# The gate columns of an input projection as Strassen block products: two of seven inside the attention, five behind it

## The chip, the cores and the metric

One core of a Trainium2 chip runs the whole program. The metric is the device time of one execution in microseconds (us). TensorE is called PE below, VectorE DVE, ScalarE ACT, GpSimd POOL and the queue of SyncE SP; every engine works through its own list of instructions in order.

## What is computed

A decoder block over 16 meta tokens and 1024 tokens of width 1024, in float32. The normalized rows h go through one projection `w_in`, whose columns feed a pooling mixer (u, z_pool), an attention of 8 heads (q, k, v, z_attn, forget gates) and two gates of 1024 columns each:

```python
h = rmsnorm(x, norm_g)
proj = einsum('bld,dn->bln', h, w_in)
u_pool, z_pool, q, k, v, z_attn, f_logit, g_pool, g_attn = split(proj)
y_pool = causal_multiscale_pool(u_pool) * silu(z_pool)
y_attn = forgetting_attention(q, k, v, log_f) * silu(z_attn)
merged = sigmoid(g_pool) * (y_pool @ w_up_pool) + sigmoid(g_attn) * (y_attn @ w_up_attn)
out = rmsnorm(x + merged @ w_out, final_norm_g)
```

## The kernel before

**Numbers in two parts.** Every product is taken on float32 operands that are split in a high part (ACT copies it to a shorter format) and a low part (the rest, a subtraction). A product is high·high + high·low + low·high, so a 512-column result over 1024 rows costs 3 × 8 = 24 matmuls of 128x512, and a chunk of 128 output columns for all 1024 tokens costs 48. `split_w` loads such a chunk of the weights (`raw`, two buffers), lets ACT make `whi` and POOL make `wlo` in four pieces of 128x256 (L128). h itself stands transposed and split in `hh` and `hl`.

**Stages.** (1) Norm, transposes and q, k, v of the first pair of heads, 0 to about 67 us. (2) The forget gates and the attention: 16 units (pair p, head e, half of the queries), up to 503.8 us. A unit with the first half of the queries has 5 key blocks, one with the second half 9. Each block has a pair of matmuls for the logits (`ps`, L549, L550), work on DVE, ACT and POOL for the maximum, the exponential, the split (`ph`, `pl`) and the row sums (`acc`), and a pair of matmuls on the values (`po`, L610). (3) Behind the attention: the rest of the projection, the pooling mixer and the two up projections, to 660.8 us. (4) The output projection and the last norm, to 756.4 us.

**What sets the order.** PE's list is written out by hand; the other lists are ordered by the compiler. In the attention PE's list is filled up with work that nothing there needs: `Fill.pull(ns)` inserts matmuls of the q, k, v chunks of the later pairs and of "free" chunks until they are worth `ns` by a small formula. Free are 4 chunks for u and 20 of the 24 chunks of za, zp, gp and ga (`f_raw`, 48 matmuls each; za, zp have 4 chunks each, gp and ga, the gates, 8 each). `f_raw` evacuates each 512 columns with ACT into `st` and stores them to a DRAM tile `sp_...`. The last 4 chunks (`left`) come behind the attention. The gates are needed late: `up_weights` reloads a gate chunk and `up` multiplies the up projection with its sigmoid.

**Names.** `acc` is the row sum of a unit on POOL, `m` the running maximum on DVE, `u` and `s` the tiles of the pooling chain, `y` the attention's result that is reloaded and gated by POOL in `attn_gate`, `rc` the reciprocal row sums, loaded in `attn_out`.

Of the kernel before, what the change touches and what calls it, by code (L numbers as in the profile page):

```python
# [14 lines left out]
D = 1024  # L15
NM = 16
# [14 lines left out]
RESERVE = 4  # L31
PJ, PT = 3, 2
PACE = 2.05
LATENCY = 1800.0
# [7 lines left out]
WARM = (4, 1)  # L42

# [10 lines left out]
def tile_hybrid_block(ctx, tc, x, meta, norm_g, w_in, b_forget, pool_w, pool_scale,  # L54
# [4 lines left out]
    w_in2 = w_in[0].rearrange("(k p) n -> p k n", p=128)  # L59
    wup_p = w_up_pool[0].rearrange("(k p) n -> p k n", p=128)  # L60
# [8 lines left out]
    gp = ctx.enter_context(tc.tile_pool(name="gp", bufs=13))  # L69
# [4 lines left out]
    psT = ctx.enter_context(tc.tile_pool(name="psT", bufs=PT, space=PS))  # L74
    G_, P_ = ExitStack(), ExitStack()
# [41 lines left out]

    def split_w(srcs, pool=None, tags=("wh", "wl")):
# [7 lines left out]
        nc.scalar.activation(hi, raw, AF.Copy)  # L126
        for k in range(0, KO, 2):
            nc.gpsimd.tensor_tensor(lo[:, k:k + 2], raw[:, k:k + 2], r32(hi[:, k:k + 2]), op=ALU.subtract)  # L128
        return hi, lo
# [176 lines left out]

    class Fill:
# [195 lines left out]
    pw = ap_.tile([128, 4, 128], F32, name="pw", tag="ls")  # L503
# [135 lines left out]
    raws = [(n, j) for n, c in (("za", 4), ("zp", 4), ("gp", 8), ("ga", 8)) for j in range(c)]  # L639

    for g in (3, 2, 1, 0):
        F.add_free(f_u(g))
# [37 lines left out]
    A.close()  # L680
    P_.close()

    bp = ctx.enter_context(tc.tile_pool(name="bp", bufs=1, reuse_waits="tile"))
    p8 = ctx.enter_context(tc.tile_pool(name="p8", bufs=3, space=PS, reuse_waits="tile"))

# [3 lines left out]
    def reload(key):  # L689
        t = btile("rl")  # L690
        nc.scalar.dma_start(t, spill[key])
        return t
# [12 lines left out]
    def pool_mm(zp, g, plh, pll):  # L705
        yh = btile("yh", F32R, "y")
        yl = btile("yl", F32R, "y")
        for c0, c1 in HALVES:
            ps = bank()
            run(g_mm3(ps, [(pwh[:, g], pwl[:, g], plh[:, c0:c1], pll[:, c0:c1])]))  # L710
            nc.vector.scalar_tensor_tensor(zp[:, c0:c1], ps, psc[:, g:g + 1], zp[:, c0:c1], op0=ALU.mult, op1=ALU.mult)
            nc.scalar.activation(yh[:, c0:c1], zp[:, c0:c1], AF.Copy)
            yls.append(nc.gpsimd.tensor_tensor(yl[:, c0:c1], zp[:, c0:c1], r32(yh[:, c0:c1]), op=ALU.subtract))
        ypl[g] = (yh, yl)

    def attn_in(p):
        y = gp.tile([128, SEQ], F32, name="y", tag="g")
        nc.sync.dma_start(y, spill["y", p])
        Y[p] = y

    def attn_gate(p, zs):
        ins = nc.gpsimd.tensor_tensor(Y[p], Y[p], zs, op=ALU.mult)
        if p > 1:
            after(ins, yls[-1])

    def attn_out(p):
        rc = btile("rc")
        for e in range(2):
            rw = recs.rearrange("(h c) r -> h (c r)", h=H)[4 * e + p:4 * e + p + 1]
            after(nc.sync.dma_start(rc[rows(e)[0]], rw.to_broadcast([64, SEQ])), stores[-1])  # L730
# [7 lines left out]
    def pool_chain(g):  # L738
        u = gp.tile([128, L], F32, name="u", tag="g")
# [4 lines left out]
        bufs2 = [gp.tile([128, L], F32, name="s2", tag="g") for _ in range(2 if g else 1)]  # L744
# [10 lines left out]
        chains[g] = u, gp.tile([128, SEQ], F32R, name="plh", tag="g"), gp.tile([128, SEQ], F32R, name="pll", tag="g")  # L755
# [7 lines left out]
    pool_chain(3)  # L763
    pool_chain(2)
    zp, za = [], []
    for z, key in ((zp, "zp"), (za, "za")):
        for g in range(4):
            z.append(reload((key, 3 - g if key == "zp" else g)))
    zp.reverse()
    left = [f_raw(key, cols[key[0]] + 128 * key[1]) for key in raws]  # L770

    def half_raw(g):
        for _ in range(3 * KO + 1):
            next(g)

    def pooled(g):
        pool_mm(zp[g], g, *chains[g][1:])

    mg, gt, ya = [], {}, []

    def up_weights(j, a):
# [6 lines left out]
        sg_ = reload((("gp", "ga")[a], j))  # L788
        return wh, wl, sg_

    def up(j, a, ws):
# [3 lines left out]
        if a:  # L795
            gh = gp.tile([128, SEQ], F32R, name="gh", tag="g")
            gl = gp.tile([128, SEQ], F32R, name="gl", tag="g") if j < 5 else btile("gl", F32R)
            mg.append((gh, gl))
        for c0, c1 in HALVES:
# [4 lines left out]
            if a:  # L804
                nc.vector.tensor_tensor(sg_[:, c0:c1], sg_[:, c0:c1], gt[j][:, c0:c1], op=ALU.add)
                nc.scalar.activation(gh[:, c0:c1], sg_[:, c0:c1], AF.Copy)  # L806
                nc.gpsimd.tensor_tensor(gl[:, c0:c1], sg_[:, c0:c1], r32(gh[:, c0:c1]), op=ALU.subtract)  # L807
# [3 lines left out]
    for p in range(3):  # L811
        attn_in(p)
    half_raw(left[0])
    pool_split(3)
    run(left[0])
    split2 = pool_split(2)
    silu(zp[3])
    silu(zp[2])
    fin = sm.tile([128, 384], F32, name="fin", tag="fz", bufs=1)
    lall = fin[:, :256].rearrange("p (u a j) -> p u a j", u=4, a=4)  # L820
    rall = fin[:, 256:320]
    rect = fin[:, 320:].rearrange("p (b r) -> p b r", b=2)
    for p in range(4):
        nc.sync.dma_start(lall[32 * p:32 * p + 32],
                          sums[4 * p:4 * p + 4].rearrange("u (a r) j -> r u a j", r=32))
    after(nc.vector.tensor_reduce(rall.rearrange("p (u j) -> p u j", u=4), lall.rearrange("p u a j -> p u j a"),
                                  axis=AX.X, op=ALU.add), split2)
    nc.vector.reciprocal(rall, rall)
    nc.vector.transpose(fin[:, 320:], rall)
    nc.sync.dma_start(recs.rearrange("(b p) r -> p b r", p=128), rect)  # L830
    pool_chain(1)
    half_raw(left[1])
    silu(zp[1])
    silu(zp[0])
    run(left[1])
    pooled(3)
    silu(za[0])
    silu(za[1])
    attn_gate(0, za[0])
    pool_split(1)  # L840
    pool_chain(0)
    attn_in(3)
    half_raw(left[2])
    silu(za[2])
    silu(za[3])
    attn_gate(1, za[1])
    run(left[2])
    pooled(2)
    pool_split(0)
    half_raw(left[3])  # L850
    first_up = up_weights(0, 0)
    pooled(1)
    pooled(0)
    run(left[3])
    attn_gate(2, za[2])
    HX.close()
    hq = ctx.enter_context(tc.tile_pool(name="hq", bufs=16, side="right", reuse_waits="tile"))
    attn_gate(3, za[3])
# [13 lines left out]
    up(0, 0, first_up)  # L872
    for p in range(4):
        attn_out(p)
    up(1, 0, second_up)
    for j in range(8):
        if j < 6:
            up(j + 2, 0, up_weights(j + 2, 0))
        up(j, 1, up_weights(j, 1))
        if j in (2, 3, 4, 5):  # L880
            wo_chunk(j - 2)
    for k in range(4, 8):
        wo_chunk(k)
    fgb = btile("fgb", F32, "y")
# [9 lines left out]
    def out_tile(i, parts):  # L894
        r = slice(i * 128, (i + 1) * 128)
        xr = btile("xr", F32, "y")
        sq = btile("sq", F32, "y")
# [59 lines left out]
```

## Time and profile before

| | |
|---|---|
| median of three runs | 759.65 us (757.79 to 760.47) |
| the profiled execution | 758.1 us, of which span 756.4 us |
| PE busy | 744.6 us (98%), 3746 matmuls |
| DVE, ACT, POOL busy | 489.0, 370.4, 307.8 us |
| DMA | 79.54 MB |

How to read it: matmuls overlap, so the duration in a row is longer than the distance from one matmul to the next; the pace is read from starts. Busy time of the other engines is occupancy. An engine's idle time matters only where the chain that ends last runs through it.

### The profile page before, as it was taken

The page shows a single profiled execution, that of the slowest core. Times are in us where ns is not written, and L with a number is a line of the kernel's source. Part 1 is how long each engine was busy: PE and PEld are TensorE (multiplying, and loading weights), DVE is VectorE, ACT ScalarE, POOL GpSimd, SP SyncE. Part 2 cuts the span into 40 slices and gives each one's busy share as a digit, 9 for nine tenths or more (in the row PEclk, how much of TensorE's full clock was granted, in tenths as well). Part 3 has the DMA queues.
Part 4 walks back from the last instruction along what each step waited for, and adds up shares of the span by engine and source line. Part 5 has one row for each costly group of instructions (what it writes and reads, how often), then busy time and mean ns, then how long its engine had stood idle before and what let it go on. Part 6 is the DMA issues. An engine that isn't in the chain of part 4 may idle for free.

```text
span 756.4 us, 10583 instructions
## 1 busy us (share of the span) xinstructions
PE 744.6 (98%) x3746; PEld 633.6 (84%) x3746; DVE 489.0 (65%) x935; ACT 370.4 (49%) x708; POOL 307.8 (41%) x338
## 2 busy tenths in 40 slices
PE   8999999999999999999999999999999999999996
PEld 5997999998898898898988888888888788888885
DVE  4753667768779787698697766891566555534322
ACT  6662456446557555575565445531745553313112
POOL 4331336446416544544364354453573123213111
PEclk9999999999999999999999999999999999999999
DMA  9201132221221222221223322349447663523231
GB/s 312 71 20 38 29 94 75 72 85 50 78 61 45 80 63 70 83 60 50 74 66 105 98 74 78 91 149 339 136 168 208 236 196 102 177 84 132 91 112 55
DMA packets 78151, 79.54 MB, mean 105 GB/s; under 512 B 9857, under 2 KB 61057, under 8 KB 78098
## 3 DMA queue, kind: packets, MB, share of 16 engines
q1 hardware_dynamic: 73344, 63.65, 27.6%
q10 hardware_dynamic: 4754, 15.21, 5.9%
q8 instruction: 29, 0.48, 0.3%
q14 instruction: 24, 0.20, 0.1%
HBM read 57.68 MB, written 21.17 MB: 104 GB/s over the span
## 4 chain that ended last, share of the span: by engine, by line
PE 90%; DVE 3%; issue 1%; ACT 0%; POOLq 0%; POOL 0%; DVEq 0%; ACTq 0%
PE pj L139 67%; PE pj L891 12%; PE po L610 5%; PE ps L550 3%; PE ps L549 2%; PE pj L463 1%; PE pj L256 0%; DVE rl L803 0%; DVE yal L735 0%; DVE S L589 0%; DVE y L731 0%; DVE m L565 0%; ACT S L558 0%; DVE ka L243 0%; DVE xt L176 0%
## 5 line engine op out<-in xcount | busy, mean ns | idle before, releaser
L128 POOL TENSOR_TENSOR wlo<-raw,whi 128x256 fp32r<-128x256 f32 x148 | 121.8, 853 | 199.2 <-ACT whi L126 103.9
L139 PE MATMUL pj<-hh,whi 128*128 128x512 f32 (+4 forms) x768 | 178.9, 361 | 0.2 <-DVE V L262 0.2
L139 PE MATMUL pj<-hl,whi 128*128 128x512 f32 (+4 forms) x768 | 177.1, 359 | 0.0
L139 PE MATMUL pj<-hh,wlo 128*128 128x512 f32 (+4 forms) x768 | 174.7, 359 | 0.0
L139 PEld LDWEIGHTS pj<-hh,wlo 128*128 128x128 f32 x768 | 132.4, 188 | 18.2
L139 PEld LDWEIGHTS pj<-hh,whi 128*128 128x128 f32 x768 | 132.2, 189 | 18.0 <-PE pj L256 0.4
L139 PEld LDWEIGHTS pj<-hl,whi 128*128 128x128 f32 x768 | 131.6, 188 | 17.7
L594 DVE TENSOR_TENSOR pl<-S,ph 128x512 fp32r<-128x512 f32 (+4 forms) x112 | 86.8, 790 | 18.8 <-ACT ph L593 18.2
L602 POOL TENSOR_TENSOR acc<-acc,S 128x272 f32<-128x272 f32 (+4 forms) x80 | 76.4, 955 | 9.8 <-ACT S L590 4.7
L558 ACT ACTIVATE S<-ps,negc 128x400 f32<-128x400 f32 (+2 forms) x96 | 49.3, 515 | 45.1 <-DVE S L556 35.8
L590 ACT ACTIVATE S<-S 128x512 f32<-128x512 f32 (+4 forms) x112 | 49.5, 478 | 32.2 <-DVE S L589 32.0
L593 ACT ACTIVATE ph<-S 128x512 fp32r<-128x512 f32 (+4 forms) x112 | 52.2, 480 | 15.8 <-PE po L610 14.5
L565 DVE TENSOR_TENSOR m<-m,S 128x272 f32<-128x272 f32 (+4 forms) x80 | 41.4, 518 | 23.9 <-ACT S L558 22.2
L294 ACT ACTIVATE st<-pj 128x512 f32<-128x512 f32 x48 | 28.5, 594 | 50.9 <-PE pj L139 28.9
L589 DVE TENSOR_TENSOR S<-S,pt 128x512 f32<-128x512 f32 (+4 forms) x112 | 51.9, 498 | 0.8
L891 PE MATMUL pj<-woh,gl 128*128 128x512 f32 (+1 forms) x136 | 51.9, 382 | 0.0
L891 PE MATMUL pj<-wol,gh 128*128 128x512 f32 (+1 forms) x136 | 51.9, 381 | 0.0
L891 PE MATMUL pj<-woh,gh 128*128 128x512 f32 (+1 forms) x136 | 51.7, 380 | 0.0
L126 ACT ACTIVATE whi<-raw 128x1024 fp32r<-128x1024 f32 x37 | 39.1, 1056 | 25.1 <-PE pj L139 23.3
L807 POOL TENSOR_TENSOR gl<-rl,gh 128x512 fp32r<-128x512 f32 x16 | 22.3, 1396 | 70.9 <-ACT gh L806 70.9
L803 DVE TENSOR_TENSOR rl<-pj,rl 128x512 f32<-128x512 f32 x32 | 22.0, 689 | 31.3 <-PE pj L139 28.0
L556 DVE SCALAR_TENSOR_TENSOR S<-ps,negc,mask 128x128 f32<-128x128 f32 (+2 forms) x72 | 23.7, 330 | 23.0 <-PE ps L550 22.2
(165 smaller groups left out, 1107.4 us busy)
## 6 DMA issues: line engine op xcount, KB each, us to landing
raw<-in_w_in_dram SPq DMA_DIRECT2D x40, 512.0 KB, 3.9
sp_gp<-st SPq DMA_DIRECT2D x16, 256.0 KB, 2.0
sp_ga<-st SPq DMA_DIRECT2D x16, 256.0 KB, 2.0
rl<-sp_gp ACTq DMA_DIRECT2D x8, 512.0 KB, 4.7
rl<-sp_ga ACTq DMA_DIRECT2D x8, 512.0 KB, 4.3
rawo<-in_w_out_dram SPq DMA_DIRECT2D x8, 512.0 KB, 4.2
xr<-in_x_dram SPq DMA_DIRECT2D x8, 512.0 KB, 4.1
xt<-in_x_dram SPq DMA_DIRECT2D x7, 512.0 KB, 7.7
```

What stands on the lines that cost most here:

```text
L126: nc.scalar.activation(hi, raw, AF.Copy)
L128: nc.gpsimd.tensor_tensor(lo[:, k:k + 2], raw[:, k:k + 2], r32(hi[:, k:k + 2]), op=ALU.subtract)
L139: nc.tensor.matmul(ps, a, b, start=(i == 0), stop=(i == len(seq) - 1))
L558: nc.scalar.activation(s[:kb, f0:], ps[:kb, f0:], AF.Identity, bias=nb_)
L565: nc.vector.tensor_tensor(m[:kb, c0:], m[:kb, c0:], s[:kb, c0:], op=ALU.max)
L589: nc.vector.tensor_tensor(s[:kb, c0:], s[:kb, c0:], self.pm[:kb, c0:], op=ALU.subtract)
L590: exps.append(nc.scalar.activation(s[:kb, c0:], s[:kb, c0:], AF.Exp))
L593: nc.scalar.activation(ph[:kb, c0:], s[:kb, c0:], AF.Copy)
L594: dves.append(nc.vector.tensor_tensor(pl[:kb, c0:], s[:kb, c0:], r32(ph[:kb, c0:]), op=ALU.subtract))
L602: nc.gpsimd.tensor_tensor(acc[:kb, c0:], acc[:kb, c0:], s[:kb, c0:], op=ALU.add)
L610: nc.tensor.matmul(self.po[:, c0:], v, r[:kb, c0:], start=(b == 0 and i == 0), stop=(b == self.nb - 1 and i == 1))
L891: nc.tensor.matmul(ps[:, :c1 - c0], mg[k][a][:, r], wo[k][b][:, c0:c1], start=(k == 0 and n == 0), stop=(k == KO - 1 and n == 2))
```

## The change

The 16 gate chunks form 8 pairs n of neighbours. A pair over 1024 tokens and 1024 rows is a 2x2 block product (two chunks of columns, two halves of the rows, two halves of the tokens), and Strassen's scheme in Winograd's form takes it with seven products of 12 matmuls in place of eight.

- Weights: `f_comb` (32 tasks: 8 pairs, 4 row groups k) loads two pieces of 128x2x128, makes four combinations with four instructions on POOL (128x128 each) and stores them to DRAM, `comb[n]` (named `sd_...` in the order). One tile `q` serves all tasks in turn. They are free fill without matmuls, so the compiler puts them where it sees room: 11 stand ahead of the first unit, 21 in the units.
- In the attention: `f_mix` (8 times) takes one chunk of za or zp whole (48 matmuls) and, for one pair, the two products on unchanged blocks (24 matmuls, the first stored alone in `xone`). It replaces the 20 `f_raw`. `pull` counts only `RATE` = 0.78 of what it is asked.
- Behind it: `minus` builds four combinations of the blocks of h (`tone`, `tthree`, `ttwo`, `tfour`; three of them written over blocks of `hh` and `hl`), each over four row groups k: x = difference of highs, y = difference of lows, x + y, then a copy on ACT and a subtraction. k < `TK` = 3 is on DVE, k = 3 on POOL in pieces of 128x256. `prep` loads and splits the weights (Z and X for a pair, M for two), and `third`, `fives`, `sixes` are the five products and the additions of the results, on DVE from PSUM. 40 products of 12 matmuls stand here; 4 chunks of 48 stood here before.
- Moved: the pooling matmuls come behind all products; the y tiles are loaded and gated once the memory of h is free; gate tiles are reloaded by SP in place of ACT's queue; POOL's subtractions of 512 or more columns are cut in pieces of 256.

```diff
-    for _ in range(24 - RESERVE):
-        key = raws.pop(0)
-        F.add_free(f_raw(key, cols[key[0]] + 128 * key[1]))
+    tasks = [f_comb(n, k) for n in range(8) for k in range(4)]
+    for n, key in enumerate(raws):
+        add_tasks(4)
+        F.add_free(f_mix(n, key, cols[key[0]] + 128 * key[1]))
+    F.add_free(f_early())
...
         def pull(self, ns):
-            self.debt += ns
+            self.debt += RATE * ns
...
+    def g_prod(ps, W, B, start=True):
+        for a, b in ((0, 0), (0, 1), (1, 0)):
+            for k in range(4):
+                nc.tensor.matmul(ps, W[a][:, k], B[b][k], start=start and n == 0, stop=n == 11,
+                                 skip_group_check=True)
...
+    def minus(o, a, b, k, eng):
...
+        sub(x, ah, bh)
+        sub(y, al, bl)
+        sub(x, x, y, ALU.add)
+        nc.scalar.activation(oh, x, AF.Copy)
+        sub(ol, x, r32(oh))
...
+    prep(0)
+    for o, a, b in ((tone, b12, b11), (tthree, b22, b12), (ttwo, b22, tone), (tfour, b21, ttwo)):
+        for k in range(4):
+            minus(o, a, b, k, nc.vector if k < TK else nc.gpsimd)
+    third(0)
+    third(1)
+    prep(1)
+    third(2)
+    third(3)
+    fives(0)
+    fives(1)
+    prep(2)
+    sixes(0)
+    sixes(1)
...
+    first_up = up_weights(0, 0)
+    for p in range(4):
+        attn_in(p)
+        attn_gate(p, za[p])
```

**POOL at the end of the attention.** Before, from the last additions of the last unit on, only the splits of weight chunks follow (`wlo`), each of them four pieces:

```order
L602 TENSOR_TENSOR acc<-acc,S 128x144 [waits Activation_49,Pool_49]
L602 TENSOR_TENSOR acc<-acc,S 128x16 [waits Activation_49,Pool_49]
L128 TENSOR_TENSOR wlo<-raw,whi 128x256 [waits DMAHW6_49,PE_49,Activation_49]
L128 TENSOR_TENSOR wlo<-raw,whi 128x256 x3
L128 TENSOR_TENSOR wlo<-raw,whi 128x256 [waits DMAHW3_49,PE_49,Activation_49]
L128 TENSOR_TENSOR wlo<-raw,whi 128x256 x3
```

Now, from the second split behind the attention on (wlo_5426 belongs to the second M, wlo_5462 and wlo_5472 to Z and X of pair 0, tm_5496 and the write to hl0 to `tone`, k = 3):

```order
L123 TENSOR_TENSOR wlo_5426<-raw_5422,whi_5425 128x256 [waits DMAHW6_49,PE_49,Activation_49]
L123 TENSOR_TENSOR wlo_5426<-raw_5422,whi_5425 128x256
L123 TENSOR_TENSOR wlo_5426<-raw_5422,whi_5425 128x256 [waits DMAHW7_49]
L123 TENSOR_TENSOR wlo_5462<-raw_5458,whi_5461 128x256 [waits DMAHW5_49,DVE_49,Activation_49]
L123 TENSOR_TENSOR wlo_5462<-raw_5458,whi_5461 128x256 [waits DMAHW7_49]
L123 TENSOR_TENSOR tm_5496<-hh0_112 128x256 [waits DVE_49]
L123 TENSOR_TENSOR tm_5496<-hl0_114 128x256 x2
L123 TENSOR_TENSOR tm_5496<-tm_5496 128x256 [waits Pool_49] x2
L123 TENSOR_TENSOR wlo_5472<-raw_5468,whi_5471 128x256 [waits DMAHW1_49,Activation_49]
L123 TENSOR_TENSOR hl0_114<-tm_5496,hh0_112 128x256 [waits Activation_49]
L123 TENSOR_TENSOR hl0_114<-tm_5496,hh0_112 128x256 [waits Pool_49]
```

What moved: POOL's list now holds the fourth row group of each block between the weight splits. In the same manner, and with no gap in the list, follow Z of pair 1, one piece of its X, the first six pieces of `tthree`, the rest of X, Z of pair 2, the two last pieces of `tthree`, then `ttwo` around X of pair 2, Z of pair 3, and `tfour`, with an addition to xu ahead of its two last pieces. From wlo_5426 to the last piece of `tfour` these are 64 pieces of 128x256 and one instruction of 128x512.

**PE at the same place.** Before, the fill of the attention runs on into the remaining chunks:

```order
L610 MATMUL po<-pl,V 128x16 [waits DVE_49]
L139 MATMUL pj<-hh_112,whi 128x512
L139 MATMUL pj<-hh_113,whi 128x512 x4
L139 MATMUL pj<-hl_114,whi 128x512 x4
L139 MATMUL pj<-hl_115,whi 128x512 x4
L139 MATMUL pj<-hh_112,wlo 128x512 x4
L139 MATMUL pj<-hh_113,wlo 128x512 x4
```

Now four products of 12 on unchanged blocks (`third`) come behind the fill, and then, shown here, the first two on built blocks (`fives` of pair 0, on `tone` and `tthree`):

```order
L330 MATMUL pj<-hh_112,whi 128x512 [waits Activation_49] x4
L330 MATMUL pj<-hl_114,whi 128x512 [waits DVE_49] x3
L330 MATMUL pj<-hl_114,whi 128x512 [waits Pool_49]
L330 MATMUL pj<-hh_112,wlo 128x512 x4
L330 MATMUL pt<-hh_112,whi 128x512 [waits Activation_49] x4
L330 MATMUL pt<-hl_114,whi 128x512 [waits DVE_49] x3
L330 MATMUL pt<-hl_114,whi 128x512 [waits Pool_49]
L330 MATMUL pt<-hh_112,wlo 128x512 x4
```

What moved: each first use of a built block waits for ACT, for DVE and, for k = 3, for POOL. `fives` of pair 1 stands next, then `sixes` of pair 0, whose two products are the first uses of `ttwo` and `tfour` and wait in the same way.

More of the change, by code (lines that the diff above doesn't have):

```diff
@@ L680, in tile_hybrid_block @@
     A.close()
+    GP.close()
     P_.close()
@@ L743, in pool_chain @@
         step = 1
-        bufs2 = [gp.tile([128, L], F32, name="s2", tag="g") for _ in range(2 if g else 1)]
+        bufs2 = [cp.tile([128, L], F32, name="s2", tag="c", bufs=3) for _ in range(2 if g else 1)]
         i = 0
@@ new lines, in tile_hybrid_block @@
+    b11, b21, b12, b22 = blk(0, 0), blk(1, 0), blk(0, 1), blk(1, 1)
+    two = [so.tile([128, 4, 512], F32R, name="t2", tag="t2", bufs=2) for _ in range(2)]
+    tone, tthree, ttwo, tfour = b11, b12, [[t[:, k] for k in range(4)] for t in two], b21
+    for n in range(4):
+        x_load(n)
+    prep(0)
[3 more added lines that the diff above has]
+    third(0)
```

306 lines of the change are left out of this document (216 added, 90 removed).

## The prediction

> **What bounds the kernel now.** I read the page's busy times, the chain that ends last, what PE waited for, and then the time by stage.
>
> ```profile
> PE 744.6 (98%) x3746; PEld 633.6 (84%) x3746; DVE 489.0 (65%) x935; ACT 370.4 (49%) x708; POOL 307.8 (41%) x338
> PE 90%; DVE 3%; issue 1%; ACT 0%; POOLq 0%; POOL 0%; DVEq 0%; ACTq 0%
> PE pn L364 <- DVE car L497: 1.3, 1, 1.3
> 519.72 2.02 PE L139 MATMUL pj<-hh,whi 128*128 128x512 f32 x8
> 521.57 2.02 PE L139 MATMUL pj<-hl,whi 128*128 128x512 f32 x8
> 503.80 74.54 PE pj L139 x321
> ```
>
> PE is the bound: 90% of the chain is its own, and the longest entry of what it waited for is 1.3 us. Two groups of eight full matmuls start 521.57 − 519.72 = 1.85 us apart, 0.2315 us each; I price every 128x512 matmul so (busy durations overlap and read longer). The last row is PE running through the 192 left gate matmuls and more without a break.
>
> Attention, by unit: first the eight units with 9 blocks in their softmax part ("odd"), then the first and last of the seven others ("even"). Columns: length, then busy PE, PEld, DVE, ACT, POOL, granted clock, DMA.
>
> ```profile
> 117.00:145.00 28.00, 28.00 (x177) 27.48 (x176) 19.64 (x47) 15.41 (x32) 18.16 (x17) 1.00 0.28 81
> 168.90:197.30 28.40, 28.18 (x149) 24.16 (x148) 22.66 (x50) 15.41 (x35) 15.59 (x16) 1.00 0.22 61
> 221.10:249.20 28.10, 28.06 (x149) 24.59 (x148) 26.07 (x52) 17.23 (x35) 16.04 (x17) 1.00 0.22 62
> 273.10:300.80 27.70, 27.70 (x136) 23.14 (x135) 22.43 (x50) 15.39 (x35) 15.72 (x16) 1.00 0.24 72
> 324.70:352.60 27.90, 27.90 (x151) 25.18 (x151) 25.20 (x52) 19.05 (x39) 16.48 (x16) 1.00 0.17 43
> 376.50:404.30 27.80, 27.80 (x130) 22.92 (x130) 23.96 (x48) 14.38 (x31) 15.59 (x16) 1.00 0.29 81
> 428.20:455.80 27.60, 27.60 (x127) 22.79 (x127) 21.36 (x45) 14.63 (x29) 15.69 (x16) 1.00 0.28 82
> 479.70:503.50 23.80, 23.80 (x107) 19.46 (x106) 21.08 (x30) 12.67 (x25) 15.61 (x16) 1.00 0.30 88
> 145.00:168.90 23.90, 23.90 (x127) 21.27 (x126) 15.82 (x34) 12.24 (x25) 12.15 (x15) 1.00 0.30 87
> 455.80:479.70 23.90, 23.90 (x112) 19.80 (x111) 16.57 (x36) 11.87 (x24) 9.44 (x13) 1.00 0.31 95
> sum 167.20, PE 167.20 PEld 144.42 DVE 118.18 ACT 88.89 POOL 65.43; mean PE 23.89 PEld 20.63 DVE 16.88 ACT 12.70 POOL 9.35
> ```
>
> PE fills every unit; DVE is close behind in the odd ones (up to 26.07 of 28.10) and has room in the even ones (mean 16.88 of 23.89).
>
> **The sum's base.** Rows come from one execution of 758.1 us, 1.5 below the median of 759.65; I add 1.5 at the end.
>
> **1. Fewer matmuls.** The gates take 16 x 48 = 768 matmuls now and 8 x 7 x 12 = 672 after: 96 x 0.2315 = **−22.2 us**, the whole gain that there can be. Where they stand matters as much: the attention's free chunks fall from 20 x 48 = 960 to 8 x 72 = 576 (−88.9 us), and behind it 4 x 48 = 192 become 40 x 12 = 480 (+66.7).
>
> **2. The attention: less cover for DVE.** Of an odd unit of 27.9 us some 4.6 are PE's own attention matmuls (12 full ones, 2.8, and 16 narrower ones by their columns), the rest is fill. With 0.78 of the fill PE needs 4.6 + 0.78 x 23.3 = 22.8, the last unit, without logits, 3.2 + 0.78 x 20.6 = 19.3; an even unit 4.6 + 0.78 x 19.3 = 19.7. DVE's work there stays. If it never idled, the odd units would exceed PE by 3.3 + 2.4 + 1.2 + 1.8 (26.07, 25.20, 23.96, last 21.08) = 8.7 us; at the 93% that it reached in its fullest unit (26.07/28.10) by 5.3 + 4.4 + 3.0 + 3.4 and, for 22.66, 22.43 and 21.36, 1.6 + 1.4 + 0.2 = 19.3 us. Waits of PE in an odd unit are not made up in an even one, since `po` stands in PE's list in order; but DVE's room may take some. POOL gets 21 of the 32 `f_comb` tasks there, 84 instructions of 128 columns; nearest rows:
>
> ```profile
> L602 POOL TENSOR_TENSOR acc<-acc,S 128x144 f32<-128x144 f32 x16 | 11.0, 685 | 1.3
> L594 DVE TENSOR_TENSOR pl<-S,ph 128x512 fp32r<-128x512 f32 x48 | 50.5, 1066 | 10.9 <-ACT ph L593 10.6
> L589 DVE TENSOR_TENSOR S<-S,pt 128x512 f32<-128x512 f32 x48 | 31.6, 681 | 0.6
> ```
>
> At most 84 x 0.685 = 58 us on an engine that is half idle: not a bound, but pl, which reads two SBUF tensors, takes 1066 ns where S (one operand from PSUM) takes 681, and a busier POOL makes more of DVE's work so. I take **+14**, ends 4 and 25.
>
> **3. The opening: +2 (0 to 4).** Eleven tasks stand among the norm's `rstd` on POOL, each waiting for two loads and the store of the one before. An rstd behind them may come a few us late, and DVE's scaling and PE's transposes after it:
>
> ```profile
> 27.04 1.41 DVE L176 SCALAR_TENSOR_TENSOR xt<-xt,rstd,gb 128x512 f32<-128x512 f32 x2 [0.67 <-POOL rstd L110]
> 31.10 0.60 PE L187 MATMUL pt<-ident,xt 128*128 128x128 f32 x4
> 39.22 1.41 DVE L176 SCALAR_TENSOR_TENSOR xt<-xt,rstd,gb 128x512 f32<-128x512 f32 x2 [0.66 <-POOL rstd L110]
> 41.56 0.60 PE L187 MATMUL pn<-ident,xt 128*128 128x128 f32 x4
> ```
>
> The transposes start 2.6 us (31.10 − 28.45) and 0.9 us (41.56 − 40.63) after the scaling ends; that is the slack. `f_comb` moves 32 x 512 KB, 16 MB, on DMA engines busy 0.17 to 0.31 in the units: no cost.
>
> **4. Behind the attention: POOL's queue.** T is the end of the fill. PE has the four `third` (48 matmuls, 11.1 us), then four `fives`, one product of `sixes` on `ttwo`, one on `tfour`: 10 x 12 x 0.2315 = 27.8 us to the end of the tenth, if nothing waits. The tenth needs `tfour`, k = 3, and POOL has 64 pieces and one 512-column addition ahead of that, gated at T: the second M reuses a buffer that the last fill matmul reads. What a piece costs:
>
> ```profile
> L128 POOL TENSOR_TENSOR wlo<-raw,whi 128x256 fp32r<-128x256 f32 x148 | 121.8, 853 | 199.2 <-ACT whi L126 103.9 <-issue 37.5 <-ACT S L558 25.2
> 218.95 2.81 POOL L128 TENSOR_TENSOR wlo<-raw,whi 128x256 fp32r<-128x256 f32 x4 [12.02 <-issue]
> 390.96 3.96 POOL L128 TENSOR_TENSOR wlo<-raw,whi 128x256 fp32r<-128x256 f32 x4
> 508.90 5.50 POOL L128 TENSOR_TENSOR wlo<-raw,whi 128x256 fp32r<-128x256 f32 x4 [8.95 <-ACT whi L126]
> 508.49 2.93 DVE L748 TENSOR_TENSOR s<-s 128x1037 f32<-128x1037 f32 x2
> L126 ACT ACTIVATE whi<-raw 128x1024 fp32r<-128x1024 f32 x37 | 39.1, 1056 | 25.1 <-PE pj L139 23.3 <-issue 1.2 <-POOL wlo L128 0.5
> ```
>
> Four pieces take 2.81 us at best (0.70 each), 3.96 (0.99) in the crowded attention, and 5.50 (1.375) against DVE's long sums. DVE does 48 such 512-column instructions in this stretch, so the best case is excluded as a mean; I take the group's mean, 0.85. The chain: 1.3 (ACT's whi and its signal) + 64 x 0.85 + 1.3 (the addition) + 1.2 (five matmuls left) = 58.2 after T, 30.4 later than PE could be: **+30**. At 0.70 it is 48.6 and +21; at 0.99 67.2 and +39; at 1.375 91.8 and +64. I keep 21 to 45. DVE's twelve rows per block at 0.7 to 1.07 us (8 to 13 us) are shorter than POOL's 14 to 18 pieces and hang on them, since three tm tiles serve both. Later, 44 pieces stand against 30 products (83 us): covered, as are DVE's additions of the results there, about five per pair of some 0.7 us in 13.9 us of PE. SP's loads of raw (3.9 us) run ahead within two buffers and stay under POOL's 3 to 4 us per split.
>
> The Trainium skill speaks against the blocks too: GPSIMD Engine Reference, section Specifications, says that POOL's SBUF interface is shared with DVE and collides with DVE instructions that read two SBUF tensors. The trace agrees (5.50 against 2.81 us). If by that rule every piece met such an instruction, this term would be the 64 us above and the time 820.
>
> **5. The tail: +3 (0 to 6).** The y tiles now load only when h is free; then come gating on POOL and `attn_out`:
>
> ```profile
> y<-sp_y SPq DMA_DIRECT2D x4, 512.0 KB, 4.9
> rl<-sp_gp ACTq DMA_DIRECT2D x8, 512.0 KB, 4.7
> L722 POOL TENSOR_TENSOR y<-y,rl 128x1024 f32<-128x1024 f32 x4 | 11.0, 2766 | 0.0
> ```
>
> POOL has 16 pieces of yl and 16 of y, 22 to 28 us, and the last tile's division and split need about 3.5 more; PE's cover is 24 pooling and 96 up matmuls, 27.8 us. The gate reloads, now on SP, land in 4.7 us and go out a step of 24 matmuls (5.6 us) ahead: hidden, barely.
>
> **Sum.** −22.2 + 14 + 2 + 30 + 3 = +26.8: 758.1 + 26.8 = 784.9, with 1.5 more **786 us**. With all low ends +2.8 (762), with all high ends +57.8 (817).
>
> **Rivals.** (a) Faster: the blocks are ready in time. The one point is the pace of POOL's pieces: with every other term at its low end of 4 us the gain survives if the chain costs less than 18.2, that is under (18.2 + 27.8 − 3.8)/64 = 0.66 us a piece, or if it starts ahead of T. With 5 us of it left: −22.2 + 4 + 5 = −13.2, 746 us. For it speaks that 0.70 is seen and that DVE may idle between blocks; against it that no group of four in the trace is under 2.8 us. (b) No change: pieces at 0.70 and the attention hidden, −22.2 + 21 + 1 = about 0, 760. (c) The attention costs more: DVE bound there (25), pieces at 0.99 (39), 5 for the rest: +46.8, 806. (d) PE slows down after its waits:
>
> ```profile
> L364 PE MATMUL pn<-onesr 128*128 128x512 f32 x5 | 2.9, 695 | 1.3 <-DVE car L497 1.3
> L139 PE MATMUL pj<-hh,whi 128*128 128x512 f32 x432 | 118.0, 397 | 0.2 <-DVE V L262 0.2
> ```
>
> The first full matmuls of the program last 695 ns against 397 later, 0.3 more. If each of three waits of several us in term 4 (on `tthree`, `ttwo`, `tfour`) brings that back for about ten matmuls, it adds 9 us: 795. The granted clock is 1.00 in every window above, so the trace has no wait that would show it. The Trainium skill (TensorE: Matmul & The Clock Gate, Why this matters for your kernels) asks for no PE gaps over about 3 us, else the clock falls back to half; by that rule (d) holds, and no run shown here has such a gap.
>
> **How the numbers follow.** The sum as worked out 0.45, (c) 0.20, (d) 0.15, (b) 0.07, (a) 0.13. A change under 0.3% (2.3 us) can't be told from none here. Faster 0.13, same 0.07, slower 0.80. The range 757 to 810 leaves out (a) and a few hundredths above; a slower case alone spans 762 to 817.
>
> **What would show it.** Right: in the profile after, PE waits for POOL's pieces (hl, t2) 20 to 45 us in total behind the attention, POOL at 9 tenths there with PE below 9; in the odd units DVE over 90% and PE waiting at po for pl; PE's matmuls 96 fewer. Wrong: PE at 9 tenths throughout, which would leave 737 to 745. Most likely to fail is the pace of the pieces or the start at T: each tenth of a us per piece moves the time by 6.4.

## The result

The changed kernel takes 889.73 us (median of 4 runs, 888.79 to 890.38) against 759.03 of the kernel before: ratio 1.172, 95% interval 1.1695 to 1.1745. Slower was forecast, but by 27 us; it is 131.

The profile page of the changed kernel: busy times, tenths of PE, POOL and the granted clock in 40 slices, the chain that ended last, and the costliest new group.

```profile
PE 777.9 (88%) x3650; PEld 646.0 (73%) x3650; DVE 573.7 (65%) x1027; ACT 380.8 (43%) x724; POOL 445.8 (50%) x586
PE   9889986987995799889898994659899789999997
POOL 4453358457554674525364379975752902261211
PEclk9989988898997989999898996669999889999999
PE 38%; DVE 12%; POOL 8%; issue 5%; ACT 3%; DMA 2%; SPq 0%; POOLq 0%; DVEq 0%; ACTq 0%
L364 POOL TENSOR_TENSOR q<-q 128x128 f32<-128x128 f32 x128 | 65.2, 509 | 128.7 <-DMA q<-in_w_in_dram 121.5
```

PE has its 96 fewer matmuls (3746 to 3650), yet its busy time grew by 33 us (744.6 to 777.9): its matmuls ran at a lower granted clock, 0.922 on average (0.999 before). PE's own share of the chain fell from 90% to 38%. The last row is the one to stop at: 65 us of `f_comb` work on POOL, and 121.5 us more in which POOL stood in front of it for its loads.

The units of the attention, answering to the rows of before (columns as there): the three longest units, and the sums of the eight odd and of the seven even ones; then the whole stretch from the first unit's end to the last's.

```profile
125.30:163.40 38.10, 28.76 (x140) 26.43 (x139) 23.61 (x48) 14.71 (x32) 24.58 (x33) 0.82 0.41 111
263.60:298.00 34.40, 23.26 (x103) 17.74 (x102) 18.37 (x40) 12.83 (x28) 19.55 (x32) 0.85 0.39 104
298.00:328.30 30.30, 26.10 (x134) 23.58 (x133) 26.14 (x52) 15.42 (x34) 22.96 (x30) 0.89 0.32 92
sum 213.30, PE 192.72 PEld 166.62 DVE 175.69 ACT 119.58 POOL 134.60; mean PE 24.09 PEld 20.83 DVE 21.96 ACT 14.95 POOL 16.82
sum 182.00, PE 153.99 PEld 128.06 DVE 129.48 ACT 84.53 POOL 80.63; mean PE 22.00 PEld 18.29 DVE 18.50 ACT 12.08 POOL 11.52
125.30:520.60 395.30, 346.71 (x1665) 294.68 (x1664) 305.17 (x623) 204.11 (x436) 215.23 (x284) 0.93 0.34 94
```

The attention got longer (395.3 us for these 15 units, 386.5 before) with 384 fewer fill matmuls in it. DVE, which I had watched and forecast at over 90% in the odd units, is at 82% there (175.69 of 213.30 us): it isn't full.

To say where time goes I use one measure in all runs, worked out from the trace: for each matmul the distance to the next one's start, less the pace of its width at full clock in the kernel before (0.232 us at 512 columns, 0.175 at 384, 0.126 at 272, and so on). What PE needs fell from 720.0 to 697.7 us; what it loses, by waits and by a lower clock, rose from 28.5 to 182.3. By stage (opening: to 60 us; attention: to its last matmul; blocks: from there to the end of the tenth product; rest):

| run | us | opening | attention | blocks | rest |
|---|---|---|---|---|---|
| before | 759.0 | 14.8 | 11.7 | – | 2.0 |
| after | 889.7 | 22.1 | 100.0 | 41.7 | 18.5 |
| nocomb | 840.2 | 14.4 | 51.5 | 48.4 | 19.4 |
| comb_nopool | 839.9 | 15.6 | 58.5 | 41.8 | 17.9 |
| comb_wait | 847.3 | 19.5 | 59.8 | 42.2 | 18.2 |
| comb_work | 843.1 | 14.3 | 61.3 | 41.8 | 18.4 |
| comb_nodma | 883.7 | 47.4 | 69.4 | 42.1 | 17.7 |
| spread | 885.4 | 23.5 | 86.0 | 48.4 | 19.3 |
| spread2 | 859.2 | 13.8 | 70.5 | 48.1 | 18.3 |
| nocomb_noblk | 796.7 | 15.0 | 50.1 | 2.3 | 19.9 |
| nocomb_rate1 | 851.4 | 16.3 | 67.7 | 44.7 | 16.3 |
| cover (89.1 more needed) | 861.3 | 14.5 | 27.6 | 1.5 | 18.8 |
| spread_tk4 | 874.6 | 21.8 | 88.5 | 35.8 | 21.4 |
| keepwarm (14.9 more needed) | 882.7 | 22.3 | 96.6 | 26.3 | 15.0 |
| tail_yh | 888.0 | 23.8 | 97.0 | 41.8 | 18.4 |
| tail_dve | 886.1 | 23.5 | 97.0 | 42.2 | 18.0 |
| combo (14.9 more needed) | 844.1 | 14.6 | 66.5 | 19.6 | 19.2 |

### The profile page after: what moved, and what is told of

Its sections match the earlier page's. It is cut to its first block, busy times and chain, and to the rows that moved or that the text cites. A ratio compares the mean times of both kernels' runs of the same rounds, so it can differ in the third digit from the quotient of the medians.

```text
span 888.0 us, 11075 instructions
## 1 busy us (share of the span) xinstructions
PE 777.9 (88%) x3650; PEld 646.0 (73%) x3650; DVE 573.7 (65%) x1027; ACT 380.8 (43%) x724; POOL 445.8 (50%) x586
## 4 chain that ended last, share of the span: by engine, by line
PE 38%; DVE 12%; POOL 8%; issue 5%; ACT 3%; DMA 2%; SPq 0%; POOLq 0%; DVEq 0%; ACTq 0%
PE pj L149 15%; PE pj L1079 10%; PE pj L330 7%; POOL wlo L123 3%; PE pt L330 3%; POOL tm L123 3%; PE po L672 2%; DVE S L651 2%; DVE pl L656 1%; DVE my L639 1%; POOL yl L123 1%; DVE tm L930 1%; PE ps L611 1%; PE ps L612 1%; ACT ph L655 1%
## 5 line engine op out<-in xcount | busy, mean ns | idle before, releaser
L123 POOL TENSOR_TENSOR wlo<-raw,whi 128x256 fp32r<-128x256 f32 x196 | 163.4, 864 | 90.7 <-ACT whi L137 79.3
L364 POOL TENSOR_TENSOR q<-q 128x128 f32<-128x128 f32 x128 | 65.2, 509 | 128.7 <-DMA q<-in_w_in_dram 121.5
L149 PE MATMUL pj<-hh,wlo 128*128 128x512 f32 (+4 forms) x512 | 116.2, 356 | 8.7 <-POOL wlo L123 8.7
L149 PE MATMUL pj<-hh,whi 128*128 128x512 f32 (+4 forms) x512 | 118.9, 359 | 5.6 <-ACT whi L137 4.5
L149 PE MATMUL pj<-hl,whi 128*128 128x512 f32 (+4 forms) x512 | 117.9, 360 | 0.0
L149 PEld LDWEIGHTS pj<-hh,wlo 128*128 128x128 f32 x512 | 90.4, 200 | 18.0 <-POOL wlo L123 9.9
L149 PEld LDWEIGHTS pj<-hh,whi 128*128 128x128 f32 x512 | 90.2, 201 | 15.0 <-ACT whi L137 5.3
L149 PEld LDWEIGHTS pj<-hl,whi 128*128 128x128 f32 x512 | 92.0, 204 | 8.8
L656 DVE TENSOR_TENSOR pl<-S,ph 128x512 fp32r<-128x512 f32 (+4 forms) x112 | 80.3, 730 | 20.1 <-ACT ph L655 19.2
L611 PE MATMUL ps<-qa,ka 128*128 128x512 f32 (+4 forms) x112 | 39.9, 356 | 20.5 <-ACT S L620 20.2
L627 DVE TENSOR_TENSOR m<-m,S 128x272 f32<-128x272 f32 (+4 forms) x80 | 44.7, 559 | 19.4 <-ACT S L620 17.4
L330 PE MATMUL pj<-hh,whi 128*128 128x512 f32 x152 | 46.3, 413 | 11.5 <-ACT hh L939 11.5
L1079 PE MATMUL pj<-wol,gh 128*128 128x512 f32 (+1 forms) x136 | 51.5, 379 | 0.0
```

Of the source, the lines that this page charges most:

```text
L123: ins = nc.gpsimd.tensor_tensor(out[:, c:c + 256], x[:, c:c + 256], y[:, c:c + 256], op=op)
L149: nc.tensor.matmul(ps, a, b, start=(i == 0), stop=(i == len(seq) - 1))
L330: nc.tensor.matmul(ps, W[a][:, k], B[b][k], start=start and n == 0, stop=n == 11, skip_group_check=True)
L364: nc.gpsimd.tensor_tensor(o, x, y, op=op)
L656: dves.append(nc.vector.tensor_tensor(pl[:kb, c0:], s[:kb, c0:], r32(ph[:kb, c0:]), op=ALU.subtract))
L1079: nc.tensor.matmul(ps[:, :c1 - c0], mg[k][a][:, r], wo[k][b][:, c0:c1], start=(k == 0 and n == 0), stop=(k == KO - 1 and n == 2))
```

## The experiments

**Without f_comb, without the blocks.** `nocomb` takes plain columns of `w_in` for all products; `nocomb_noblk` leaves out the building of the blocks as well.

```diff
-    tasks = [f_comb(n, k) for n in range(8) for k in range(4)]
+    tasks = []
...
-        ops["Z", n] = split_w([comb[n][:, 2], comb[n][:, 3]], **kw)
+        ops["Z", n] = split_w([wc(n, 2), wc(n, 3)], **kw)
```

```diff
-    for o, a, b in ((tone, b12, b11), (tthree, b22, b12), (ttwo, b22, tone), (tfour, b21, ttwo)):
-        for k in range(4):
-            minus(o, a, b, k, nc.vector if k < TK else nc.gpsimd)
```

> Leaves out the sums of weight columns: no f_comb at all (its 64 loads, 128 POOL subtractions and 32 stores); the products take plain columns of w_in straight from their tensor. Theory W (waits: each f_comb task holds POOL's and SP's in-order queues for a round trip of some 7 us, and splits, acc and stores stand behind it): PE's lost time between 60 and 520 us, about 100 us now, falls to the 15 to 40 that I had priced, 889.7 - 60 to 85 = 805 to 830. Theory D (DVE bounds the attention because the fill was thinned to 0.78): 880 to 890. Theory P (POOL's additions slow DVE at the shared SBUF side): 815 to 835, told apart by the run that keeps the additions.

> As the run without f_comb, and the four blocks are not built either (the 16 row differences, on DVE and POOL): the products read the plain blocks of hh and hl. Left are the 96 fewer matmuls, the new order and the tail. If the transition's loss (some 42 us between 520 and 600) is the wait for the blocks, 40 to 50 us under the run without f_comb: 760 to 790. If it is the loads and splits of the weights that stand ahead there, only 5 to 15 under it.

Measured: 840.2 (ratio to before 1.1056, 1.1033 to 1.1079) and 796.7 (1.0485, 1.0463 to 1.0506). f_comb costs 49.5 us, less than theory W asked and far more than D. (The attention and the opening lose 48.5 and 7.7 less without it, the blocks 6.7 more.) The blocks cost 43.5, in the stage where they are waited for (48.4 lost, then 2.3). And 796.7 is still 60 over 737, what the fewer matmuls alone would leave.

**What of f_comb costs: its loads and stores, its work, or its wait.** Four runs, each keeping one part.

```diff
# comb_nopool: no subtraction
-            nc.gpsimd.tensor_tensor(o, x, y, op=op)
+            pass
# comb_wait: one subtraction of two columns, which needs both loads and holds the store
+        nc.gpsimd.tensor_tensor(q[:, 0, :2], q[:, 0, :2], q[:, 3, :2], op=ALU.add)
# comb_nodma: a tile that stays, no load, no store
-            nc.sync.dma_start(q[:, 2 * i:2 * i + 2], w_in4[:, :, k, c:c + 128])
...
-        nc.sync.dma_start(comb[n][:, :, k], q)
# comb_work: as comb_nodma, and each task held in its place
+            ins = nc.gpsimd.tensor_tensor(o, x, y, op=op)
+            if o is d and last_pool:
+                after(ins, last_pool[-1])
```

> Keeps f_comb's loads and stores through the one tile q, leaves out the 128 POOL subtractions (so plain columns come back). Theory W: POOL's queue is freed but SP's still stands at each store for its load and at each load for the store before, so a part of the gain: 830 to 870; near 820 if only POOL's queue mattered, near 885 if only SP's did. Theory P: 815 to 835. Theory D: 880 to 890.

> Keeps the 128 POOL subtractions of f_comb, at the same places, on one tile that stays in SBUF; leaves out its loads and stores, and the products take plain columns of w_in. Theory W: within 10 us of the run without f_comb (815 to 840), since nothing waits any more. Theory P: no better than the changed kernel, 875 to 890. Theory D: 880 to 890.

> f_comb with its loads and stores through the one tile q at the old places; of its four POOL subtractions of 128 columns only one of two columns is left, which still needs both loads and which the store still needs (so plain columns come back, a few of them summed). POOL's work for f_comb falls from 65 to about 2 us, its standing for the round trip stays (some 120 us idle in front of it). If the standing in POOL's queue is the 45 to 50 us that f_comb costs: 875 to 890. If the work is: 838 to 850.

> The 128 POOL subtractions on one tile that stays in SBUF, no loads, no stores (products take plain columns of w_in), as in the earlier run, but each task now held behind the POOL instruction that was emitted last, so that they stand along the attention and not in the opening. Work kept, round trip gone. If the round trip is the cost: 840 to 852. If the work or its collision with DVE is: 872 to 890.

`comb_nopool` 839.9: the 16 MB of loads and stores and SP's queue cost nothing by themselves. `comb_nodma` 883.7 looked like proof that the work is the cost, and isn't; its tenths of PE and POOL show why:

```profile
PE   6427999989998999899898994569899789999997
POOL 7987312654545454536364479975761802251211
```

With no load to wait for, the scheduler put the subtractions into the opening, POOL at 7 to 9 tenths there, and PE lost 47.4 us in the first 60 instead of 22.1. The run measured another place. With the tasks held in place (`comb_work`) the same work costs 2.9 us over `nocomb` (1.1073 to 1.1109; the two intervals overlap); and the wait with nearly no work (`comb_wait`) 7.1. Theories W and P fall as they stood: neither the standing nor the work costs much alone, together they cost 49.5.

POOL's time between 100 and 200 us tells how that is. First the changed kernel, in three views: the busy time of each engine (PE, PEld, DVE, ACT, POOL, then clock and DMA), of POOL on the tile q alone, and POOL's wait for q's loads (total, times, longest).

```profile
100.00:200.00 100.00, 83.29 (x446) 78.40 (x445) 66.08 (x142) 47.73 (x105) 54.05 (x83) 0.88 0.37 97
```

```profile
100.00:200.00 100.00, 23.52 (x44) 0.88 0.37 97
```

```profile
POOL q L364 <- DMA q<-in_w_in_dram: 46.2, 10, 7.5
```

Then the first view of the run without f_comb, the three of `comb_wait`, and the first two of `comb_work`, which has no such wait:

```profile
100.00:200.00 100.00, 96.36 (x549) 88.84 (x548) 83.97 (x180) 55.46 (x125) 50.93 (x56) 0.98 0.24 68
```

```profile
100.00:200.00 100.00, 92.43 (x536) 85.12 (x535) 78.69 (x173) 58.42 (x129) 49.78 (x67) 1.00 0.50 134
```

```profile
100.00:200.00 100.00, 3.50 (x14) 1.00 0.50 134
```

```profile
POOL q L361 <- DMA q<-in_w_in_dram: 45.1, 11, 6.3
```

```profile
100.00:200.00 100.00, 92.86 (x523) 85.51 (x522) 81.65 (x170) 52.59 (x119) 69.53 (x95) 0.97 0.22 62
```

```profile
100.00:200.00 100.00, 22.49 (x40) 0.97 0.22 62
```

In the changed kernel POOL is busy for 54.05 and stands for 46.2 of 100 us (a wait at the edge of the window counts whole): its in-order queue is full. f_comb holds 23.5 + 46.2 = 69.7 of it, and 30.5 are left for acc, wlo and the rest, which at PE's pace without f_comb need 50.9. With the wait alone 46.3 get through, with the work alone 47.0: nearly enough. So the cost appears where work plus standing pass the queue's slack, and then fill and softmax work behind it wait for POOL. The changed kernel's waits show both. From 100 to 200 us DVE's softmax step at L618 waits twice for `acc` on POOL, 4.3 and 3.3 us; and from 110 to 480 us PE's fill waits for `wlo`. `nocomb` has neither entry in these windows.

```profile
PE pj L149 <- POOL wlo L123: 8.7, 2, 6.1
```

One rival stays in part. SP's queue, which issues these loads and stores, stands at them for 65.9 of the 100 us in the changed kernel. It does so for 55.0 in `comb_nopool` and 55.7 in `comb_wait`, which hardly cost anything, so its standing alone is not the cause; no run separates what the longer standing adds beside a full POOL queue.

**Taking the wait away in the whole computation.** `spread` loads a task 12 fill matmuls ahead of its subtractions; `spread2` does so with two tiles q and holds each task in place.

```diff
-        q = ap_.tile([128, 4, 128], F32, name="q")
+            q = ap_.tile([128, 4, 128], F32, name="q", bufs=2)
...
+    def spread_out(g):
+        for i, c in enumerate(g):
+            yield c
+            if i % 12 == 11 and tasks:
+                tasks.pop(0)()
```

> The whole computation; f_comb in two halves: the loads of a task at one point of the fill, its four subtractions and its store 12 fill matmuls later, one half at every 12th matmul of f_u and f_mix, so that POOL rarely waits for a load; work and DMAs are the same. The two runs before told: without POOL's part of f_comb 840, with loads and stores but no subtractions 840 as well. If the 50 us are the standing of POOL's queue for the round trip (121.5 us idle in front of L364 in the changed kernel): 840 to 855. If they are the 65 us of POOL work itself, or its collision with DVE: 875 to 890.

> The whole computation; f_comb in halves as in the run before, with two tiles q (the row of norm weights of the opening moves to another tile to make room) and each task's first subtraction held behind the POOL instruction emitted last, so that its loads are a task ahead. In the run with one tile POOL still stood 117 us for q's loads, so that run did not take the wait away. If the wait is the cost and the idle time in front of f_comb falls to under 30 us here: 840 to 855; with half of it left 860 to 870; if the work is the cost: 875 to 890.

`spread` 885.4, but POOL's waits show that the edit did not do what I meant:

```profile
POOL q L371 <- DMA q<-in_w_in_dram: 117.2, 30, 6.8
```

One tile means that a load can't start before the store of the task before; in POOL's list the next task's subtractions often stand directly behind the last one's. So this run says nothing on work against wait. `spread2` cut that entry and came to 859.2 (1.1302, 1.1281 to 1.1324):

```profile
POOL q L374 <- DMA q<-in_w_in_dram: 27.8, 8, 7.3
```

That is 30.6 of the 49.5 back, with all the work done, but 4 us over the range expected for under 30 us of waits. Of the 19 left I can name only these 27.8 us of waits; what they cost, and the rest, isn't settled.

**The attention's own loss.** `nocomb` still loses 51.5 us there (11.7 before). `nocomb_rate1` pulls the fill at its full rate; `cover` gives the fill of `nocomb_noblk` its 960 matmuls back, 384 of them with zero weights, pulled at the full rate as before the change.

```diff
-RATE = 0.78
+RATE = 1.0
# cover, besides:
+                if n == 1:
+                    for _ in range(more):
+                        nc.tensor.matmul(ps, zero, B[0][0], start=False, stop=False, skip_group_check=True)
```

> As the run without f_comb (840.2), with the fill pulled at its full rate, 1.0 for 0.78: the units get as many fill matmuls as before the change, and the fill is used up by about unit 12. If the attention's remaining loss (some 40 us) comes from the thin cover: the early units lose nothing, the last four have nothing beside them and pay it there, so within 10 us, 830 to 850. If DVE bounds the attention whatever the fill: the same. If the 0.78 itself cost time (PE waiting with fill in store): 800 to 825.

> As the run without f_comb and without blocks (796.7), with 384 matmuls of zero weights added to the products in the attention (24 in each of the 16), so that the attention's free fill is 960 matmuls again as before the change, pulled at the full rate. They are 88.9 us of PE work. If the attention lost its time to the thin cover, they fill waits: PE at 9 tenths to the attention's end and 25 to 50 us slower, 822 to 847. If the attention's losses have another cause (DVE, POOL, loads), the whole 88.9 come on top: 875 to 890.

`nocomb_rate1` 851.4: from 100 to 420 us PE loses some 19 us where `nocomb` loses 35, but the fill ends at 423 us, and between 420 and 480 us alone PE loses 43. So a higher rate only moves the loss; whether the amount is the cause, the other run tells. `cover` 861.3: 64.6 more for 89.1 more needed, so 24.5 us were free, between the two expectations. The rows from 100 to 460 us of `nocomb_noblk` and of `cover`:

```profile
100.00:460.00 360.00, 342.26 (x1740) 293.89 (x1738) 305.97 (x628) 203.86 (x437) 178.25 (x205) 0.99 0.27 76
```

```profile
100.00:460.00 360.00, 359.01 (x1836) 313.28 (x1836) 246.96 (x525) 182.34 (x381) 156.04 (x179) 1.00 0.22 63
```

With the old amount PE is full there (359 of 360) and loses 9 us in this stretch, not 40; 17 us come back between 500 and 540, where the fill is used up before the last unit is done. So the thin cover is shown to be the cause of most of the 40 us that the attention loses without f_comb. It is not DVE's busy time (306 of 360): PE waits many times and briefly for the softmax steps. In `nocomb`, from 110 to 480 us, its longest entries are

```profile
PE ps L616 <- ACT S L625: 9.8, 11, 1.5
PE po L677 <- DVE pl L661: 8.4, 16, 1.1
PE po L677 <- ACT ph L660: 2.8, 5, 1.2
```

**The blocks.** `spread_tk4` gives all rows of the differences to DVE; `keepwarm` puts zero-weight matmuls into PE's waits on the changed kernel.

```diff
-TK = 3
+TK = 4
# keepwarm
+                if fill and not a and not b and k > 1:
+                    for _ in range(fill):
+                        nc.tensor.matmul(ps, zero, b22[0][0], start=False, stop=False, skip_group_check=True)
```

> As the run with f_comb in halves, and all four rows of each block difference on DVE (TK = 4), so POOL has 32 pieces of weight splits ahead of the tenth product, not 64, and DVE 64 operations, not 48. If POOL's chain sets the transition (52 us lost there without f_comb): DVE's 64 at 0.7 to 1.2 us are 45 to 77 us from the end of the fill, against 75 measured to the end of the tenth product, so 10 to 25 us faster than the run with TK = 3. If DVE set it already: 5 to 15 us slower.

> The whole computation of the changed kernel, with 64 more matmuls of zero weights, 8 ahead of rows 2 and 3 of the first product on each of the four blocks, where PE waits behind the attention; they add zeros. They take 15 us of PE out of some 35 of waits there. If the lower clock after the waits costs time behind the attention (rival (d), 9 us): 5 to 12 us faster. If POOL's chain hides it, since a slow PE still waits for the next block: within 4 us of 889.7.

`spread_tk4` 874.6, 10.8 under `spread`, and 12.6 less lost in that stage: POOL's chain does set it. `keepwarm` 882.7 (1.1598 to 1.165). The window from 520 to 600 us, first of the changed kernel, then of `keepwarm`:

```profile
520.00:600.00 80.00, 50.34 (x168) 35.69 (x167) 57.51 (x61) 22.96 (x33) 69.37 (x72) 0.72 0.35 108
```

```profile
520.00:600.00 80.00, 61.91 (x234) 47.36 (x233) 60.40 (x59) 23.01 (x32) 70.52 (x70) 0.89 0.37 113
```

The clock rose from 0.72 to 0.89, PE got 66 more matmuls done (64 of them the zero ones), and the stage took as long as before: 74.4 us from the attention's last matmul to the end of the tenth product, 74.7 without. The time fell as far as was expected if the clock mattered, but not in that stage: of the two profiles' difference 3.3 us lie in the attention, without a cause that I can name, and 3.5 behind the blocks. There the changed kernel has a wait of 2.52 us for `st` that ends at 643 us, and 3.4 us at half clock after it (the last section shows both), together a loss of 4.2; `keepwarm` has one wait of 0.4 us in that place. The lower clock between the attention and the tenth product is hidden by the chain of the blocks.

**The tail.** `tail_yh` orders ACT's silu of za behind the eight yh; `tail_dve` gives half of the yl to DVE.

```diff
# tail_yh
-        silu(za[g])
+        after(nc.scalar.activation(za[g], za[g], AF.Silu), yhs[-1])
# tail_dve
+            if g % 2:
                 yls.append(pool_tt(yl[:, c0:c1], zp[:, c0:c1], r32(yh[:, c0:c1]), ALU.subtract))
+            else:
+                nc.vector.tensor_tensor(yl[:, c0:c1], zp[:, c0:c1], r32(yh[:, c0:c1]), op=ALU.subtract)
```

> The changed kernel with one more order: ACT's four silu of za behind the eight yh of the pooled branch (before: the first silu stands in ACT's queue for its load, 11.1 us, and the yh, POOL's yl, 17.4 us idle, and the up matmuls stand behind it). If that silu makes the tail late: the waits for yh and yl (1.1 + 4.2 us) and the half clock after them go, 4 to 9 us faster, 881 to 886. If POOL's 32 pieces or the loads set the tail: within 3 us of 889.7.

> The changed kernel with the yl of two of the four pooled groups on DVE, so POOL has 8 pieces there, not 16 (11.1 us in a row between 686 and 697, while the first up product waits 1.1 + 4.2 us for yh and yl and then runs at half clock). If those pieces are what holds the first up product: 4 to 9 us faster, 881 to 886. If the loads of za, y and the gates hold it: within 3 us of 889.7.

888.0 (1.1665 to 1.1713, no difference) and 886.1 (1.1604 to 1.1681; 3.6 under the changed kernel, between the two expectations, from runs of 878.2 to 888.4). PE's waits from 680 to 730 us, of the changed kernel and of `tail_dve`:

```profile
PE pj L149 <- POOL yl L123: 4.2, 1, 4.2
PE pj L149 <- ACT whu L1014: 3.6, 1, 3.6
PE pj L149 <- ACT yh L794: 1.1, 1, 1.1
```

```profile
PE pj L149 <- ACT whu L1017: 5.3, 1, 5.3
PE pj L149 <- ACT yh L794: 2.6, 1, 2.6
```

The wait for yl went and the other two grew by 3.2: the stage loses 18.0 us, 18.5 before the edit. What sets the end of the tail stays open.

**All together.** `combo`: two tiles q, TK = 4, yl shared, zero-weight matmuls.

```diff
+            q = ap_.tile([128, 4, 128], F32, name="q", bufs=2)
-TK = 3
+TK = 4
+FILL = 8
...
```

> The whole computation with four edits together: f_comb in halves with two tiles q, all block rows on DVE (TK = 4), yl of two groups on DVE, and the 64 zero-weight matmuls in the waits behind the attention. Alone, against their own base, they gave 30.5, 10.8, an expected 6, and 7.0 us: if they add up, 889.7 - 54 = 835. Where DVE's longer row work and the zero-weight matmuls meet the same waits they cannot both count: 838 to 850. Not under 800 in any theory, so still slower than the kernel before.

844.1 (1.1117, 1.1087 to 1.1146): 45.7 under the changed kernel. If the first two edits give 30.6 and 10.8 here too, the other two add 4.3 together. It is the best full computation with this scheme here, and no run points to one under the kernel before.

## Why the prediction was wrong

Direction and places were right, the size was not. The differences of the table's rows, with the terms as forecast (they sum to 131.5, the spans differ by 131.6):

| term | forecast | measured |
|---|---|---|
| 1 fewer matmuls | −22.2 | −22.3 (720.0 to 697.7 needed) |
| 2 attention | +14 | +88.3: f_comb 48.5 (100.0 − 51.5), cover and the rest 39.8 (51.5 − 11.7) |
| 3 opening | +2 | +7.3, gone without f_comb |
| 4 blocks | +30 (21 to 45) | +41.7; 43.5 by leaving them out |
| 5 tail | +3 | +16.5, of which 4.2 ahead of the tail: the wait for `st` at 643 us and the half clock after it |

The step that failed is in term 2: "At most 84 x 0.685 = 58 us on an engine that is half idle: not a bound". The work itself was not sized too low (0.509 us an instruction for the 0.685 taken; 65.2 us for all 32 tasks), but I counted busy time on an in-order queue and left out its standing, 121.5 us more. Term 3 has each task "waiting for two loads and the store of the one before", and prices that only for the opening. The issues of the changed kernel (KB each, median us from issue to landing) give the round trip:

```profile
q<-in_w_in_dram SPq DMA_DIRECT2D x64, 128.0 KB, 2.7
sd<-q SPq DMA_DIRECT2D x32, 256.0 KB, 2.4
```

A load, four subtractions of 0.509 and a store are 7.1 us; the 32 tasks run from 27 to 307 us, 8.7 us each with what stands between them. In all that time POOL serves the rest only in the gaps. Durations of the same order for loads stood in the profile before, so the step could have been bounded: 32 round trips against the half of POOL that was free.

The second error in term 2: I priced the thinner cover by DVE's busy time, in the odd units alone. `cover` shows that the cover is the cause, but PE waits for a chain of ACT and DVE steps, in even units too, with DVE at 85% from 100 to 460 us without f_comb. With an end of 25 us, 40 was outside.

Term 4 held by its mechanism and its range. POOL's 64 pieces after the fill's last matmul took 61.5 us, 0.96 each where I took 0.85 (+7), and POOL waited a few us between them. The sign that I had named, 20 to 45 us of waits for POOL's pieces, came only in part. PE's rows of that stage put 9.6 us down to POOL and 20.1 to ACT's copies (0.8 of them for `t`):

```profile
PE pj L330 <- ACT hh L939: 11.5, 4, 5.1
PE pt L330 <- ACT hh L939: 7.8, 3, 4.6
PE pt L330 <- POOL hl L123: 3.9, 1, 3.9
PE pj L330 <- POOL hl L123: 3.3, 1, 3.3
PE pt L330 <- POOL t L123: 2.4, 1, 2.4
```

ACT's copies in turn waited 15.6 us for sums on POOL and 8.4 for sums on DVE; that POOL's share counts is shown by `spread_tk4`. The rows of DVE show the collision of POOL and DVE:

```profile
565.21 0.68 DVE L930 TENSOR_TENSOR tm<-hl,hl 128x512 f32<-128x512 f32 x1
566.42 0.69 DVE L930 TENSOR_TENSOR tm<-tm 128x512 f32<-128x512 f32 x1
567.02 1.23 DVE L930 TENSOR_TENSOR tm<-hh,hh 128x512 f32<-128x512 f32 x1
568.17 1.22 DVE L930 TENSOR_TENSOR tm<-hl,hl 128x512 f32<-128x512 f32 x1
```

The instruction of the first row takes 0.68 us while POOL idles (564.6 to 566.6), and 1.22 beside POOL's pieces in the last row. That agrees with the Trainium skill (GPSIMD Engine Reference, Specifications), which has POOL share its SBUF interfaces with DVE; but `comb_work` shows that 65 us of such work along the attention cost 2.9 us, so the collision was not what made the kernel slow.

Term 5 counted the 96 up matmuls as cover for POOL's yl. They aren't: the first up product reads yl of all four groups in its matmuls 5 to 8, 0.93 us (4 x 0.2315) after it starts. That accounts for the wait of 4.2 us for yl; `tail_dve` took it away and gained little, so the rest of this term stays open.

Of the rivals, (a) and (b) are out. (c) had the right place with another cause. (d) is right on the clock and wrong on the place: it falls after waits, but behind the attention, up to the tenth product, the chain of the blocks hides it. In the attention it is part of the loss: over the 395.3 us of the units the granted clock is 0.93, which is 28 us of PE's cycles at most, since PE also stood still in part of that time; no run took the clock apart from the waits there.

## What to carry to other kernels

On an in-order queue, price an added step by how long it holds the queue, standing included, and compare that with the queue's slack in that stage; work and wait that are each harmless can together fill it. When matmuls that fill another stage's waits are taken out, they give back less than their own time: here 24.5 us of 89.1 were free cover. And look where an experiment's instructions landed before reading its time: two of these runs had not tested what they were written for.

## What the hardware showed

A short wait can halve PE's clock. The changed kernel by stretches of 2 us (busy PE, PEld, DVE, ACT, POOL, then the clock), and PE's list with the matmul that ends the wait:

```profile
132.00:134.00 2.00, 1.09 (x7) 0.78 (x5) 0.28 (x1) 0.00 (x0) 0.00 (x0) 1.00 0.25 37
134.00:136.00 2.00, 0.00 (x0) 0.00 (x0) 0.00 (x0) 0.36 (x2) 0.00 (x0) 0.79 0.74 202
136.00:138.00 2.00, 0.73 (x2) 0.29 (x2) 0.75 (x2) 1.97 (x5) 1.12 (x2) 0.50 0.28 88
140.00:142.00 2.00, 2.00 (x8) 1.81 (x7) 2.00 (x4) 1.71 (x4) 1.92 (x3) 0.51 0.00 0
142.00:144.00 2.00, 2.00 (x16) 2.00 (x15) 1.72 (x5) 1.32 (x5) 1.92 (x3) 1.00 0.76 176
```

```profile
137.27 0.79 PE L672 MATMUL po<-ph,V 128*128 128x512 f32 x1 [4.17 <-ACT ph L655]
```

After 4.17 us without a matmul PE ran for 4.7 us more at 0.50: the wait cost about half as much again. A wait of 2.52 us had the same effect (0.50 in the microsecond after it), one of 2.59 had none (1.00):

```profile
289.78 0.50 PE L149 MATMUL pj<-hh,wlo 128*128 128x512 f32 x1 [2.59 <-POOL wlo L123]
...
643.00 3.13 PE L330 MATMUL pt<-t,whi 128*128 128x512 f32 x8 [2.52 <-DVE st L885]
```

```profile
290.00:291.00 1.00, 1.00 (x5) 0.82 (x5) 0.05 (x1) 0.33 (x1) 1.00 (x2) 1.00 0.81 246
...
644.00:645.00 1.00, 1.00 (x4) 0.79 (x3) 0.00 (x0) 0.00 (x0) 0.00 (x0) 0.50 1.10 361
```

The Trainium skill (TensorE: Matmul & The Clock Gate, Why this matters for your kernels) sets the limit at about 3 us of idle PE. These rows agree in kind; here 2.5 us were enough in one place and not in another. The trace suggests a reason: its clock changes only at times that are multiples of 3.41 us apart (down at 135.14 and 643.73, up at 141.97 and 647.14). The wait of 2.52 us, from 640.48 on, lies inside one such step (640.32 to 643.73), while the one of 2.59, from 287.18 on, is split by 288.75. No run tests that.
